# A hybrid decoder block on one Trainium2 core: order of the first loads, order of the weight splits at head 0, and the last rows in single-bank pieces

## The chip, the cores and the metric

The kernel runs on one core of one Trainium2 chip. The engines are named as in the profile: PE multiplies matrices (PEld loads its stationary operand), DVE and ACT work elementwise, POOL prepares small tiles, SP issues most transfers between device memory and SBUF. The metric is the device time of one launch in microseconds (us), the median of several runs; less is better.

## The reference

528 rows of tokens (16 fixed ones ahead of 512) of width 1024 pass one decoder block in float32. What is computed, cut to what matters:

```
u = rmsnorm(h); q, f, i, g, b, c, x, ga, gb = split(u @ w_in)
f = lb + (1 - lb) * sigmoid(f); k = 1 - f
o = hgrn2 recurrence over (silu(q), k, i, log f), 8 heads of 128
y_a = rmsnorm(o) * silu(g);  y_b = b * causal_conv(c * x)
h = h + (sigmoid(ga) * y_a + sigmoid(gb) * y_b) @ w_out
a, v = split(rmsnorm(h) @ w_up)
h = h + (silu(causal_conv(a) + bias) * v) @ w_down
out = rmsnorm(h)[16:]          # mean of squares over 1024, then * final_norm_w
```

## The kernel before

**Products in three parts.** Every float32 operand of a matmul is split on the chip into a high and a low part, and every product is three matmuls: high by high, high by low, low by high. For weights a **unit** (128 columns of w_in, all 1024 rows) is fetched by SP, cast to `wh` by ACT (line 100) and the rest `wl` is subtracted by DVE (line 101); `load_unit` does all of it. Later weights come as **pairs**, four blocks whose sums are used in a seven-product scheme (`pair_weights`, lines 287 to 323; the subtraction there is line 304, the additions 313, 314 and 318). That scheme also needs sums and differences of the tokens, which `combos` makes for the two halves of the contraction (jp 0 and 1): line 390 to 402 compute one (`ct`), ACT line 374 and DVE line 376 split it into `cm`. They are made a step at a time by a generator, which `some(n)` advances by n steps.

**Order.** The program is written in one stream; a framework orders the instructions of each engine from it, and each engine then works through its own queue in order, waiting by semaphores on the others.

**The start.** SP's queue fetches the parameters `par_t`, then quarters of the first two units (`heads`) and the eight token tiles `xt` in turn (lines 222 to 234). ACT scales a token tile to `uh` (line 165), DVE subtracts to `ul` (line 166), PE multiplies (lines 437 to 439). Line 173 squares the first token tile into `acc`, where the sum of squares of the tokens is gathered.

**Head 0.** After the units of head 0 the loop over `items` (lines 875 to 901) goes through what is left of the projections: first three single units of head 1, (f,1), (q,1) and (i,1), kind "s", then pairs (kind "p") and merges (kind "m"). A single unit is multiplied in two halves by `half_unit`; between them `some(99)` lets the generator of the combinations run to its end. Recurrence pieces of head 0 (lines 538 to 635) are put between the matmuls. Line 842 is a piece of the convolution, line 866 the result of (q,1).

**The end.** The down projection adds into the rows `HT` by groups of 128-wide pieces of the hidden width. For the last group of four (lines 1091 to 1111), each of four chunks of 128 rows has two halves q of 512 columns with twelve matmuls each (`down3`, lines 1044 to 1046). Both halves lie in one two-bank tile of PSUM:

```
ps = new_ps()
for q in range(2):
    o = ps[:, q * 512:(q + 1) * 512]
    ...
    dve.tensor_tensor(HT[c][q], o, HT[c][q], op=ALU.add)                      # 1098
    act.activation(junk, HT[c][q], AF.Square, accum_out=ss[:, c, q:q + 1])    # 1099
    dve.tensor_tensor(HT[c][q], HT[c][q], fw[q], op=ALU.mult)                 # 1100
dve.tensor_tensor(v, ss[:, c, :1], ss[:, c, 1:], op=ALU.add)                  # 1102
dve.tensor_scalar(v, v, 1.0 / D, EPS, op0=ALU.mult, op1=ALU.add)              # 1103
```

Then `rsqrt_of` makes the reciprocal root (lines 187 to 191), ACT and DVE scale the halves by it (lines 1108 and 1110), and SP writes them out.

Of the kernel before, what the change touches and what calls it, by code (L numbers as in the profile page):

```python
# [7 lines left out]
F32 = mybir.dt.float32  # L8
F32R = mybir.dt.float32r
I32 = mybir.dt.int32  # L10
AF = mybir.ActivationFunctionType
ALU = mybir.AluOpType
PSUM = bass.MemoryType.PSUM

P = 128
D = 1024
# [10 lines left out]
EPS = 1e-6  # L27
NCH = SEQ // P
# [29 lines left out]
def block_kernel(ctx: ExitStack, tc: tile.TileContext, xT, par, wts, pairs, ident, masks, finw, out):  # L58
    nc = tc.nc
    dve, act, pe = nc.vector, nc.scalar, nc.tensor  # L60
# [17 lines left out]
    def home(i, dtype=F32, n=528, name="t"):  # L78
        return big.tile([P, 528], dtype, name=f"{name}{i}", tag=f"b{i}")[:, :n]
# [6 lines left out]
    def fetch(parts=1):  # L86
        u = next_unit[0]
        next_unit[0] += 1
        raw = wpool.tile([P, KT, P], F32, name=f"wr{u}", tag="wr")
        n = KT // parts  # L90
        return raw, [lambda i=i: nc.sync.dma_start(raw[:, i:i + n, :], wts[u, :, i:i + n, :])
                     for i in range(0, KT, n)]

    def split_unit(raw, parts=1):
        h = whl.tile([P, KT, P], F32R, name="wh", tag="wh")
        lo = whl.tile([P, KT, P], F32R, name="wl", tag="wl")
        n = KT // parts

        def part(i):
            act.copy(h[:, i:i + n, :], raw[:, i:i + n, :])  # L100
            dve.tensor_tensor(lo[:, i:i + n, :], raw[:, i:i + n, :], h[:, i:i + n, :].bitcast(F32),  # L101
                              op=ALU.subtract)

        return h, lo, [lambda i=i: part(i) for i in range(0, KT, n)]

    def load_unit():
        raw, loads = fetch()
        h, lo, parts = split_unit(raw)
        loads[0]()
        parts[0]()  # L110
        return h, lo
# [27 lines left out]
    mains = []  # L139
    turn = [0]  # L140

    def new_ps():
        pool = mains[turn[0] // 2 % len(mains)]
        turn[0] += 1
        return pool.tile([P, 1024], F32, name="psm", tag="psm")
# [38 lines left out]
    def rsqrt_of(dst, v, pool, w, tag):  # L184
        y = pool.tile([P, w], F32, name=f"ry{tag}", tag=f"ry{tag}")
        t = pool.tile([P, w], F32, name=f"rt{tag}", tag=f"rt{tag}")
        act.activation(y, v, AF.Sqrt)
        dve.reciprocal(y, y)
        dve.tensor_tensor(t, y, v, op=ALU.mult)
        dve.scalar_tensor_tensor(t, t, -0.5, y, op0=ALU.mult, op1=ALU.mult)  # L190
        dve.scalar_tensor_tensor(dst, t, 1.5, y, op0=ALU.add, op1=ALU.mult)
# [28 lines left out]
    heads = [fetch(4) for _ in range(2)]  # L220

    def load_x(k):
        nc.sync.dma_start(xt[k], xT[k * P:(k + 1) * P, :])

    nc.sync.dma_start(par_t, par)
    heads[0][1][0]()
    load_x(0)
    heads[1][1][0]()
    load_x(1)
    for i in range(1, 4):  # L230
# [231 lines left out]
    with tc.tile_pool(name="rp0", bufs=1) as rp:  # L462
# [19 lines left out]
        ahead = [load_unit()]  # L482
# [156 lines left out]
    def ring(tag="z", bufs=3):  # L639
        return p2.tile([P, L], F32, name=tag, tag=tag, bufs=bufs)  # L640
# [123 lines left out]
    def value(j):  # L764
        return lambda o, at: act.copy(V_t[:, at], o)
# [47 lines left out]
    def some(n):  # L813
        for _ in range(n):
            next(work[0], None)
# [4 lines left out]
    s = ring()  # L820
# [33 lines left out]
    def forget(j):  # L854
        def sink(o, at):
            act.activation(Fs[j % 2][:, at], o, AF.Sigmoid)
            if at.start:
                keys(j)
        return sink
# [9 lines left out]
    items = [("s", forget(1)), ("s", lambda j=1: query(j)), ("s", value(1)), ("p", lambda: GA(0)), ("m", 0)]  # L869
# [6 lines left out]
    for q, (kind, arg) in enumerate(items):  # L876
        if kind == "m":
            if cur:
                cur.last()
                cur = None  # L880
            merge(arg)
            if arg + 1 < KT:
                beat[:] = [0, 6 if arg + 2 < KT else 4]
                begin(arg + 1)
        elif kind == "p":
            w = pair_weights()
            nxt = Pair(w, arg(), HL, lambda: None)
            if cur:
                cur.last()
            cur = nxt  # L890
            cur.middle()
        else:
            unit = ahead.pop() if ahead else load_unit()
            sink = arg() if arg.__name__ == "<lambda>" and arg.__code__.co_argcount == 1 else arg
            half_unit(unit, 0, sink)
            if cur:
                cur.last()
                cur = None
            some(99)
            half_unit(unit, 1, sink)  # L900
    some(99)

    ph.close()
    scan.close()
# [46 lines left out]
    with tc.tile_pool(name="rp1", bufs=1) as rp:  # L951
        acc = fp2.tile([P, LT], F32, name="acc", tag="fa")
        for k in range(KT):
            ps = mtile(mh, ml, LATE)
# [5 lines left out]
        ahead = load_unit()  # L960
        ps = new_ps()
# [20 lines left out]
    for q, (f, i) in enumerate(units):  # L982
        unit = ahead
        if q + 1 < len(units):
            ahead = load_unit()
# [11 lines left out]
    HT = [[xt[4 * q + c][:, :512] for q in range(2)] for c in range(NCH)]  # L997
# [31 lines left out]
    n = 0  # L1029
# [11 lines left out]
    def down3(o, g, c, w, first, last):  # L1041
        gh, gl = (x[:, c * P:(c + 1) * P] for x in gs[g])
        wh, wl = w
        pe.matmul(o, gh, wh, start=first, stop=False)  # L1044
        pe.matmul(o, gh, wl, start=False, stop=False)  # L1045
        pe.matmul(o, gl, wh, start=False, stop=last)  # L1046
# [32 lines left out]
        for _ in work:  # L1079
            pass  # L1080
    pairs_ps.close()
    mains.append(ctx.enter_context(tc.tile_pool(name="pmain2", bufs=2, space=PSUM)))

    fw = [home(24 + q, n=512, name="fw") for q in range(2)]
    for q in range(2):
        nc.scalar.dma_start(fw[q], finw[q * 512:(q + 1) * 512].partition_broadcast(P))
    tp = ctx.enter_context(tc.tile_pool(name="tp", bufs=1, side="right"))
    ss = tp.tile([P, NCH, 2], F32, name="ssf")
    junk = tp.tile([P, 512], F32, name="junkf")
    grp = spans[-1]  # L1090
    ws = [[down_block() for _ in grp] for q in range(2)]
    for c in range(NCH):
        ps = new_ps()
        for q in range(2):
            o = ps[:, q * 512:(q + 1) * 512]
            for g, w in zip(grp, ws[q]):
                down3(o, g, c, w, g == grp[0], g == grp[-1])
            dve.tensor_tensor(HT[c][q], o, HT[c][q], op=ALU.add)
            act.activation(junk, HT[c][q], AF.Square, accum_out=ss[:, c, q:q + 1])
            dve.tensor_tensor(HT[c][q], HT[c][q], fw[q], op=ALU.mult)  # L1100
        v = tp.tile([P, 1], F32, name="vf", tag="vf", bufs=2)
        dve.tensor_tensor(v, ss[:, c, :1], ss[:, c, 1:], op=ALU.add)
        dve.tensor_scalar(v, v, 1.0 / D, EPS, op0=ALU.mult, op1=ALU.add)
        rf = tp.tile([P, 1], F32, name="rf", tag="rf", bufs=2)
        rsqrt_of(rf, v, tp, 1, "f")
        for q in range(2):
            if q:
                act.activation(HT[c][q], HT[c][q], AF.Copy, scale=rf)
            else:
                dve.tensor_scalar(HT[c][q], HT[c][q], rf, None, op0=ALU.mult)  # L1110
            nc.sync.dma_start(out[c * P:(c + 1) * P, q * 512:(q + 1) * 512], HT[c][q])


def _masks():
# [64 lines left out]
```

## Time and profile before

| | |
|---|---|
| median of 3 runs | 881.46 us (880.99 to 881.69) |
| profiled execution | 881.89 us |
| span of its trace | 880.1 us |
| PE busy | 862.0 us (98%), 6984 matmuls |
| DVE busy | 717.9 us (82%), 1320 instructions |
| ACT busy | 528.9 us (60%), 1002 instructions |
| POOL busy | 34.6 us (4%) |

The span is counted from the first to the last record of the trace; 1.8 us of the execution lie around it. In the timelines a row has start, duration (both us), engine, line, operation, what is written and read by the program's names, sizes, and in brackets how long the engine was idle just before and what ended that. Matmuls overlap, so their pitch (from start to start) tells more than their duration. Names in rows: `pr`, `psm`, `psq` are tiles in PSUM, `wr` a raw weight unit, `wt` the rest of a pair, `hn` normed tokens, `cacc` the convolution, `xr` rows of `HT`, `vf` the mean of squares.

### The profile page before, as it was taken

The page shows a single profiled execution, that of the slowest core. Times are in us where ns is not written, and L with a number is a line of the kernel's source. Part 1 is how long each engine was busy: PE and PEld are TensorE (multiplying, and loading weights), DVE is VectorE, ACT ScalarE, POOL GpSimd, SP SyncE. Part 2 cuts the span into 40 slices and gives each one's busy share as a digit, 9 for nine tenths or more (in the row PEclk, how much of TensorE's full clock was granted, in tenths as well). Part 3 has the DMA queues.
Part 4 walks back from the last instruction along what each step waited for, and adds up shares of the span by engine and source line. Part 5 has one row for each costly group of instructions (what it writes and reads, how often), then busy time and mean ns, then how long its engine had stood idle before and what let it go on. Part 6 is the DMA issues. An engine that isn't in the chain of part 4 may idle for free.

```text
span 880.1 us, 17447 instructions
## 1 busy us (share of the span) xinstructions
PE 862.0 (98%) x6984; PEld 814.5 (93%) x6984; DVE 717.9 (82%) x1320; ACT 528.9 (60%) x1002; POOL 34.6 (4%) x110
## 2 busy tenths in 40 slices
PE   8989999999999999999999999999999999999995
PEld 8979999999999999999999999999999999999984
DVE  7899998988988889889986559976877787877665
ACT  8854777676776667776684346554545545455424
POOL 1220020100101001020000000000000000000000
PEclk9998999999999999999999999999999999999999
DMA  7316344343443434334335323533443534433202
GB/s 255 98 34 206 121 146 127 93 155 107 144 132 88 145 116 145 107 110 145 96 94 174 97 73 95 168 99 118 147 140 108 179 98 152 135 115 125 97 24 96
DMA packets 38817, 107.98 MB, mean 123 GB/s; under 512 B 4304, under 2 KB 5712, under 8 KB 38736
## 3 DMA queue, kind: packets, MB, share of 16 engines
q1 hardware_dynamic: 38448, 106.34, 38.2%
q8 instruction: 55, 0.90, 0.4%
q10 hardware_dynamic: 288, 0.52, 0.2%
q14 instruction: 26, 0.21, 0.1%
HBM read 104.75 MB, written 2.10 MB: 121 GB/s over the span
## 4 chain that ended last, share of the span: by engine, by line
PE 79%; DVE 12%; DMA 4%; ACT 3%; issue 1%; SPq 1%; DVEq 0%; ACTq 0%
PE pr L330 14%; PE pr L331 13%; PE pr L332 13%; PE psm L1044 5%; PE psm L1046 5%; PE psm L1045 5%; PE psm L123 4%; PE psm L120 4%; PE psm L121 4%; DMA wt<-in_pairs 4%; DVE wl L304 3%; PE pr L437 3%; PE pr L439 2%; PE pr L438 2%; PE psq L544 1%
## 5 line engine op out<-in xcount | busy, mean ns | idle before, releaser
L330 PE MATMUL pr<-cm,wh 128*128 128x264 f32 (+1 forms) x784 | 228.0, 292 | 1.1 <-ACT c L338 0.9
L331 PE MATMUL pr<-cm,wh 128*128 128x264 f32 (+1 forms) x784 | 222.6, 284 | 0.0
L332 PE MATMUL pr<-cm,wl 128*128 128x264 f32 (+1 forms) x784 | 222.3, 284 | 0.0
L330 PEld LDWEIGHTS pr<-cm,wh 128*128 128x128 f32 x784 | 147.4, 188 | 6.0 <-ACT c L338 2.7
L332 PEld LDWEIGHTS pr<-cm,wl 128*128 128x128 f32 x784 | 147.8, 189 | 0.0
L331 PEld LDWEIGHTS pr<-cm,wh 128*128 128x128 f32 x784 | 147.5, 188 | 0.0
L303 ACT CAST wh<-wt 128x1024 fp32r<-128x1024 f32 x88 | 92.7, 1053 | 74.2 <-PE pr L331 34.2
L304 DVE TENSOR_TENSOR wl<-wt,wh 128x1024 fp32r<-128x1024 f32 x88 | 107.1, 1217 | 30.2 <-ACT wh L303 30.2
L101 DVE TENSOR_TENSOR wl<-wr,wh 128x1024 fp32r<-128x1024 f32 (+1 forms) x64 | 71.7, 1123 | 38.6 <-ACT wh L100 37.2
L100 ACT CAST wh<-wr 128x1024 fp32r<-128x1024 f32 (+1 forms) x64 | 61.8, 969 | 67.7 <-PE psm L121 31.1
L330 PE MATMUL pr<-cf,wh 128*128 128x258 f32 x256 | 72.5, 283 | 0.0
L331 PE MATMUL pr<-cf,wh 128*128 128x258 f32 x256 | 72.1, 282 | 0.0
L332 PE MATMUL pr<-cf,wl 128*128 128x258 f32 x256 | 71.9, 281 | 0.0
L338 ACT COPY c<-pr 128x264 f32<-128x264 f32 (+1 forms) x132 | 49.4, 374 | 30.5 <-PE pr L332 22.1
L304 DVE TENSOR_TENSOR wl<-wr,wh 128x1024 fp32r<-128x1024 f32 x44 | 53.7, 1221 | 12.0 <-ACT wh L303 11.3
L303 ACT CAST wh<-wr 128x1024 fp32r<-128x1024 f32 x44 | 46.2, 1050 | 21.1 <-PE pr L331 19.6
L313 DVE TENSOR_TENSOR wt<-wt 128x1024 f32<-128x1024 f32 x44 | 53.6, 1219 | 4.9 <-DMA wt<-in_pairs 4.8
L330 PE MATMUL pr<-cb,wh 128*128 128x258 f32 x192 | 54.7, 285 | 0.3 <-ACT xr L1005 0.3
L331 PE MATMUL pr<-cb,wh 128*128 128x258 f32 x192 | 54.7, 285 | 0.0
L332 PE MATMUL pr<-cb,wl 128*128 128x258 f32 x192 | 54.4, 283 | 0.0
L331 PEld LDWEIGHTS pr<-cf,wh 128*128 128x128 f32 x256 | 48.6, 190 | 0.8
L330 PEld LDWEIGHTS pr<-cf,wh 128*128 128x128 f32 x256 | 48.1, 188 | 0.7
(298 smaller groups left out, 2241.1 us busy)
## 6 DMA issues: line engine op xcount, KB each, us to landing
wr<-in_wts SPq DMA_DIRECT2D x56, 512.0 KB, 3.6
wr<-in_pairs SPq DMA_DIRECT2D x44, 512.0 KB, 4.1
wt<-in_pairs SPq DMA_DIRECT2D x44, 512.0 KB, 4.0
wt<-in_pairs SPq DMA_DIRECT2D x88, 256.0 KB, 4.7
xt<-in_xT SPq DMA_DIRECT2D x8, 264.0 KB, 4.5
xr<-in_xT SPq DMA_DIRECT2D x8, 264.0 KB, 3.9
out<-xr SPq DMA_DIRECT2D x8, 256.0 KB, 2.2
wr<-in_wts SPq DMA_DIRECT2D x8, 128.0 KB, 4.3
```

The lines of the kernel that those rows point to most:

```text
L100: act.copy(h[:, i:i + n, :], raw[:, i:i + n, :])
L101: dve.tensor_tensor(lo[:, i:i + n, :], raw[:, i:i + n, :], h[:, i:i + n, :].bitcast(F32), op=ALU.subtract)
L303: act.copy(h, src)
L304: dve.tensor_tensor(lo, src, h.bitcast(F32), op=ALU.subtract)
L313: dve.tensor_tensor(t[:, 1:3, :], t[:, 1:3, :], t[:, 3:, :].to_broadcast([P, 2, 512]), op=ALU.add)
L330: pe.matmul(ps, h[:, j], ch, start=start and j == 0, stop=False, skip_group_check=True)
L331: pe.matmul(ps, h[:, j], cl, start=False, stop=False, skip_group_check=True)
L332: pe.matmul(ps, lo[:, j], ch, start=False, stop=j == 3, skip_group_check=True)
L338: act.copy(c, r)
L1044: pe.matmul(o, gh, wh, start=first, stop=False)
L1045: pe.matmul(o, gh, wl, start=False, stop=False)
L1046: pe.matmul(o, gl, wh, start=False, stop=last)
```

## The change

Four edits. (1) The first token tile is fetched first, then the first quarter of weights, and the parameters third. (2) In the loop over `items`, when the next item is a single unit too, that unit is loaded and split before the first half of the present one is multiplied; and the generator of the combinations is advanced by one step between the halves and, where a single unit follows, by one after them, instead of to its end. (3) At the end every piece has a single-bank tile of PSUM of its own from a pool of four, the second half of the last chunk is cut in two pieces of 256 columns, and the multiplication by the final weights writes to a new tile `z` instead of over the rows that are squared. (4) The argument of the root is accumulated in `vs`, one instruction a piece, in place of an addition and a scaling at the end.

```diff
@@ -222,9 +222,9 @@
     def load_x(k):
         nc.sync.dma_start(xt[k], xT[k * P:(k + 1) * P, :])
 
+    load_x(0)
+    heads[0][1][0]()
     nc.sync.dma_start(par_t, par)
-    heads[0][1][0]()
-    load_x(0)
     heads[1][1][0]()
     load_x(1)
     for i in range(1, 4):
@@ -891,14 +891,16 @@
             cur.middle()
         else:
             unit = ahead.pop() if ahead else load_unit()
+            if items[q + 1][0] == "s":
+                ahead.append(load_unit())
             sink = arg() if arg.__name__ == "<lambda>" and arg.__code__.co_argcount == 1 else arg
             half_unit(unit, 0, sink)
             if cur:
                 cur.last()
                 cur = None
-            some(99)
+            some(1)
             half_unit(unit, 1, sink)
-    some(99)
+            some(1 if items[q + 1][0] == "s" else 99)
 
     ph.close()
     scan.close()
@@ -1079,36 +1081,41 @@
         for _ in work:
             pass
     pairs_ps.close()
-    mains.append(ctx.enter_context(tc.tile_pool(name="pmain2", bufs=2, space=PSUM)))
+    pfin = ctx.enter_context(tc.tile_pool(name="pfin", bufs=4, space=PSUM))
 
     fw = [home(24 + q, n=512, name="fw") for q in range(2)]
     for q in range(2):
         nc.scalar.dma_start(fw[q], finw[q * 512:(q + 1) * 512].partition_broadcast(P))
     tp = ctx.enter_context(tc.tile_pool(name="tp", bufs=1, side="right"))
-    ss = tp.tile([P, NCH, 2], F32, name="ssf")
+    ss = tp.tile([P, NCH, 3], F32, name="ssf")
+    vs = tp.tile([P, NCH, 3], F32, name="vsf")
     junk = tp.tile([P, 512], F32, name="junkf")
     grp = spans[-1]
     ws = [[down_block() for _ in grp] for q in range(2)]
     for c in range(NCH):
-        ps = new_ps()
-        for q in range(2):
-            o = ps[:, q * 512:(q + 1) * 512]
+        z = [home(26 + 2 * c + q, n=512, name="zf") for q in range(2)]
+        pieces = [(0, 0, 512), (1, 0, 512)] if c + 1 < NCH else [(0, 0, 512), (1, 0, 256), (1, 256, 512)]
+        for at, (q, a, b) in enumerate(pieces):
+            o = pfin.tile([P, 512], F32, name="pf", tag="pf")[:, :b - a]
             for g, w in zip(grp, ws[q]):
-                down3(o, g, c, w, g == grp[0], g == grp[-1])
-            dve.tensor_tensor(HT[c][q], o, HT[c][q], op=ALU.add)
-            act.activation(junk, HT[c][q], AF.Square, accum_out=ss[:, c, q:q + 1])
-            dve.tensor_tensor(HT[c][q], HT[c][q], fw[q], op=ALU.mult)
-        v = tp.tile([P, 1], F32, name="vf", tag="vf", bufs=2)
-        dve.tensor_tensor(v, ss[:, c, :1], ss[:, c, 1:], op=ALU.add)
-        dve.tensor_scalar(v, v, 1.0 / D, EPS, op0=ALU.mult, op1=ALU.add)
+                down3(o, g, c, [x[:, a:b] for x in w], g == grp[0], g == grp[-1])
+            h = HT[c][q][:, a:b]
+            dve.tensor_tensor(h, o, h, op=ALU.add)
+            act.activation(junk[:, :b - a], h, AF.Square, accum_out=ss[:, c, at:at + 1])
+            dve.tensor_tensor(z[q][:, a:b], h, fw[q][:, a:b], op=ALU.mult)
+            if at:
+                dve.scalar_tensor_tensor(vs[:, c, at:at + 1], ss[:, c, at:at + 1], 1.0 / D, vs[:, c, at - 1:at],
+                                         op0=ALU.mult, op1=ALU.add)
+            else:
+                dve.tensor_scalar(vs[:, c, :1], ss[:, c, :1], 1.0 / D, EPS, op0=ALU.mult, op1=ALU.add)
         rf = tp.tile([P, 1], F32, name="rf", tag="rf", bufs=2)
-        rsqrt_of(rf, v, tp, 1, "f")
+        rsqrt_of(rf, vs[:, c, at:at + 1], tp, 1, "f")
         for q in range(2):
             if q:
-                act.activation(HT[c][q], HT[c][q], AF.Copy, scale=rf)
+                act.activation(z[q], z[q], AF.Copy, scale=rf)
             else:
-                dve.tensor_scalar(HT[c][q], HT[c][q], rf, None, op0=ALU.mult)
-            nc.sync.dma_start(out[c * P:(c + 1) * P, q * 512:(q + 1) * 512], HT[c][q])
+                dve.tensor_scalar(z[q], z[q], rf, None, op0=ALU.mult)
+            nc.sync.dma_start(out[c * P:(c + 1) * P, q * 512:(q + 1) * 512], z[q])
 
 
 def _masks():
```

How this moves instructions on the engines is seen at three places. On DVE, around line 842 while head 0's recurrence is under way; `wl<-wr_...` on line 101 is the low part of a single unit, `cm` a split combination, `Q`, `K`, `T` belong to the recurrence. Before, from line 842 on:

```order
L842 TENSOR_TENSOR cacc<-cacc,z 128x264
L538 TENSOR_TENSOR qv<-Q_238,T_893 128x8x16 x2
L376 TENSOR_TENSOR cm_816<-ct,cm_815 128x528
L540 TENSOR_TENSOR qv<-qv,T_893 128x8x16
L546 TENSOR_TENSOR Q_238<-Q_238,T_893 128x8x16
L547 TENSOR_TENSOR Q_238<-qv,T_893 128x8x16
L548 TENSOR_TENSOR Q_238<-qv,T_893 128x8x16
L553 TENSOR_TENSOR TK_968<-T_893 128x8
L398 SCALAR_TENSOR_TENSOR ct<-ct,hn 128x528
L554 TENSOR_TENSOR TK_968<-T_893,TK_968 128x8
L562 COPY_PREDICATED B_235<-mk_t,psq 128x4x48
L555 TENSOR_TENSOR T_969<-T_893,TK_968 128x8
```

and, with `wl` of unit (q,1) on its last row, up to the subtraction:

```order
L556 TENSOR_TENSOR K_227<-K_227,TK_968 128x8x48
L562 COPY_PREDICATED B_235<-mk_t,psq 128x4x32
L376 TENSOR_TENSOR cm_818<-ct,cm_817 128x528
L562 COPY_PREDICATED B_235<-mk_t,psq 128x4x16
L402 TENSOR_TENSOR ct<-hn 128x528
L390 TENSOR_TENSOR ct<-hn 128x528
L101 TENSOR_TENSOR wl<-wr_1041,wh 128x1024
```

After, the same place:

```order
L842 TENSOR_TENSOR cacc<-cacc,z 128x264
L101 TENSOR_TENSOR wl<-wr_926,wh 128x1024
L376 TENSOR_TENSOR cm_816<-ct,cm_815 128x528
L538 TENSOR_TENSOR qv<-Q_238,T_893 128x8x16 x2
L546 TENSOR_TENSOR Q_238<-Q_238,T_893 128x8x16
L540 TENSOR_TENSOR qv<-qv,T_893 128x8x16
L547 TENSOR_TENSOR Q_238<-qv,T_893 128x8x16
L548 TENSOR_TENSOR Q_238<-qv,T_893 128x8x16
L553 TENSOR_TENSOR TK_974<-T_893 128x8
L398 SCALAR_TENSOR_TENSOR ct<-ct,hn 128x528
```

Line 101 has moved from behind eighteen instructions to right behind line 842; the next one (unit (i,1)) follows after line 402 of the first half, and lines 390 to 402 of the second half come later still.

Also on DVE, in the first pairs, where `Q_239`, `TK` and `T` belong to head 1's recurrence, `F_230` on line 668 is a result of the pair for head 2 and line 101 the unit (i,2). Before, from the recurrence's second step:

```order
L538 TENSOR_TENSOR qv<-Q_239,T_1536 128x16x2x4 x2
L546 TENSOR_TENSOR Q_239<-Q_239,T_1536 128x32x4
L540 TENSOR_TENSOR qv<-qv,T_1536 128x16x8
L547 TENSOR_TENSOR Q_239<-qv,T_1536 128x32x4
L548 TENSOR_TENSOR Q_239<-qv,T_1536 128x32x4
L553 TENSOR_TENSOR TK_1609<-T_1536 128x32
```

After, where these now stand:

```order
L668 TENSOR_TENSOR F_230<-pr,c_1412 128x264
L101 TENSOR_TENSOR wl<-wr_1480,wh 128x1024
L655 SCALAR_TENSOR_TENSOR Q_238<-pr,c_1475 128x264
L556 TENSOR_TENSOR K_228<-K_228,TK_1535 128x128x3
L562 COPY_PREDICATED B_234<-mk_t,psq 128x32x3
L673 TENSOR_TENSOR Q_238<-Q_238,z 128x264
L562 COPY_PREDICATED B_234<-mk_t,psq 128x32x2
L538 TENSOR_TENSOR qv<-Q_239,T_1536 128x16x2x4
L562 COPY_PREDICATED B_234<-mk_t,psq 128x32
L538 TENSOR_TENSOR qv<-Q_239,T_1536 128x16x2x4
L546 TENSOR_TENSOR Q_239<-Q_239,T_1536 128x32x4
L540 TENSOR_TENSOR qv<-qv,T_1536 128x16x8
```

The recurrence's second step, which stood ahead of lines 731, 734 and 668, now follows line 668, line 101 and the first result of the next product.

On ACT at the start of the program; `acc` is the sum of squares, `uh` a scaled token tile, `wh` a quarter of weights. Before:

```order
L100 CAST wh<-wr_90 128x256
L165 ACTIVATE uh_210<-xt_80,par_t 128x528
L100 CAST wh<-wr_91 128x256
L165 ACTIVATE uh_211<-xt_81,par_t 128x528
L100 CAST wh<-wr_90 128x256
L100 CAST wh<-wr_91 128x256
L173 ACTIVATE acc<-xt_80 128x528
L165 ACTIVATE uh_212<-xt_82,par_t 128x528
```

After:

```order
L173 ACT_TABLE_LOAD
L173 ACTIVATE acc<-xt_80 128x528
L277 ACTIVATE lbe_191<-lbe_191 128x8
L278 ACTIVATE lbe_192<-lbe_192 128x8
L100 CAST wh<-wr_90 128x256
L165 ACTIVATE uh_210<-xt_80,par_t 128x528
L100 CAST wh<-wr_91 128x256
L165 ACTIVATE uh_211<-xt_81,par_t 128x528
L100 CAST wh<-wr_90 128x256
L165 ACTIVATE uh_212<-xt_82,par_t 128x528
```

The square on line 173 has moved from behind the fourth cast to the head of the queue, and `uh_212` stands directly behind the third cast.

## Rows read from the trace of the kernel before

**Rows 1.** Waits of PE: what for, us in total, times, longest.
```profile
PE pr L439 <- DVE wl L101: 3.2, 1, 3.2
...
PE psm L1044 <- DVE vf L1103: 1.1, 1, 1.1
```

**Rows 2.** Windows: stretch, us, busy of PE PEld DVE ACT POOL, PEclk, DMA.
```profile
64.00:68.00 4.00, 2.19 (x10) 2.19 (x11) 4.00 (x7) 1.82 (x4) 2.99 (x4) 0.65 0.72 172
68.00:72.00 4.00, 4.00 (x20) 4.00 (x20) 3.37 (x8) 1.83 (x4) 0.00 (x0) 0.50 0.69 231
58.00:80.00 22.00, 18.48 (x143) 17.47 (x142) 20.03 (x41) 12.67 (x33) 5.50 (x10) 0.84 0.48 144
80.00:104.00 24.00, 23.69 (x193) 23.03 (x191) 23.47 (x54) 18.84 (x42) 0.00 (x0) 1.00 0.48 151
130.00:160.00 30.00, 29.99 (x273) 29.11 (x272) 26.75 (x52) 21.03 (x47) 0.00 (x0) 1.00 0.41 129
```

**Rows 3.** Timeline of PE, 65 to 74 us.
```profile
65.81 0.59 PE L439 MATMUL pr<-cm,wl 128*128 128x264 f32 x1 [3.20 <-DVE wl L101]
...
71.91 0.33 PE L438 MATMUL pr<-cm,wh 128*128 128x264 f32 x1
72.08 0.28 PE L439 MATMUL pr<-cm,wl 128*128 128x264 f32 x1
...
73.54 0.28 PE L439 MATMUL pr<-cm,wl 128*128 128x264 f32 x1
```

**Rows 4.** Timeline of DVE, 57 to 72 and 93 to 98 us.
```profile
57.99 0.43 DVE L842 TENSOR_TENSOR cacc<-cacc,z 128x264 f32<-128x264 f32 x1
...
64.48 1.27 DVE L101 TENSOR_TENSOR wl<-wr,wh 128x1024 fp32r<-128x1024 f32 x1
...
70.08 0.70 DVE L402 TENSOR_TENSOR ct<-hn 128x528 f32<-128x528 f32 x1
...
71.47 0.43 DVE L866 TENSOR_TENSOR Q<-pr,z 128x264 f32<-128x264 f32 x1 [0.63 <-ACT z L865]
...
94.12 0.47 DVE L538 TENSOR_TENSOR qv<-Q,T 128x128 f32<-128x128 f32 x2
...
97.34 0.17 DVE L555 TENSOR_TENSOR T<-T,TK 128x8 f32<-128x8 f32 x1
```

**Rows 5.** Timeline of SP, one issue of a pair's transfer.
```profile
70.81 0.33 SPq L293 DMA_DIRECT2D wt<-in_pairs  x1
```

**Rows 6.** Chain that ended last: start, us, engine, tile, line.
```profile
868.57 0.60 DVE xr L1098
...
872.30 0.70 DVE xr L1098
...
873.09 0.73 ACT junkf L1099 x2
...
874.64 0.17 DVE vf L1103
...
875.84 0.72 ACT xr L1108
```

**Rows 7.** Timeline of PE, last matmuls of the end.
```profile
867.70 0.40 PE L1046 MATMUL psm<-wh,gs 128*128 128x512 f32 x1
...
871.88 0.39 PE L1046 MATMUL psm<-wh,gs 128*128 128x512 f32 x1
```

**Rows 8.** Timeline of ACT, start of the program and a 256-wide instruction.
```profile
8.14 0.64 ACT L173 ACTIVATE acc<-xt 128x528 f32<-128x528 f32 x1
8.69 1.35 ACT L165 ACTIVATE uh<-xt,par_t 128x528 fp32r<-128x528 f32 x2
...
53.91 0.41 ACT L840 ACTIVATE z<-z 128x256 f32<-128x256 f32 x1
```

**Rows 9.** Timeline of PE, start of the program.
```profile
10.26 0.39 PE L438 MATMUL pr<-ul,wh 128*128 128x264 f32 x1 [0.17 <-DVE ul L166]
```

## The prediction

> **What bounds the kernel now.** I read the list of waits of PE first, because PE is busy almost all the time and the only quick gains are where it stands still. It shows one long wait, 3.20 us for the low half of a weight unit (line 101), and one of 1.13 us near the end for line 1103 [rows 1]. Next come the windows. Between 64 and 72 us the clock granted to PE is 0.65 and then 0.50, which is the 1.2 GHz level, after the stretch in which PE stood; everywhere else that I use it is 1.00 [rows 2]. The same rows say that DVE is nearly full around this place: of the 46 us from 58 to 104 it is idle for (22.00 - 20.03) + (24.00 - 23.47) = 2.50 us, while from 130 to 160 it has 3.25 us to spare. The timeline of PE gives the price of the lower clock, a pitch of 0.22 us between matmuls instead of 0.12 [rows 3]. The timeline of DVE gives the reason for the wait: the subtraction on line 101 starts at 64.48, although what it needs was there long before; other work stands ahead of it in DVE's queue [rows 4]. Last I read the chain of waits at the end [rows 6] and the first ten microseconds [rows 8, 9].
>
> **Head 0 and the next unit.** PE stops at 62.61 (65.81 less 3.20) and before that for 0.33 us on line 578, so 3.53 us are idle. Then it runs slowly: from 65.81 to 71.91 lie 27 intervals that take 6.10 us; at the later pitch, 12 intervals in 73.54 - 72.08 = 1.46, that is 0.1217 each, they would take 3.29, so 2.81 us are lost to the clock [rows 3]. Together 6.34 us is the most that this place can return.
>
> In the changed order line 101 stands right behind line 842, which starts at 57.99 and takes 0.43; the subtraction itself took 1.27 [rows 4]. So it would be done at about 59.6. PE, kept at its pitch, comes to the first product with the low half at about 60.1 by my laying of the new order, and needs it 2.5 us sooner than it got as far before; it still arrives in time by half a microsecond. The second moved subtraction, for the unit after it, I lay at 66.1 against a need at 66.9.
>
> What moves back pays. Eighteen DVE instructions that stood ahead of line 101 now run behind it. They are the combinations of tokens and the first steps of head 0's recurrence, and they are wanted by PE later. Their delay can only be made good by DVE's idle time and by work that is put off past this stretch. The idle time is 2.50 us. The order of the change puts off twelve small instructions of head 1's recurrence, from line 538 at 94.12 to line 555 at 97.34, past line 668 and the next line 101; their durations add to 2.7 us [rows 4]. That makes 5.2 us. Laying both queues instruction by instruction with the durations of the trace I get four new short waits of PE, on lines 633, 668, 101 and 544, of about 0.4, 0.2, 0.5 and 0.2 us, 1.3 in all, and so 6.34 - 1.3 = 5.0 us. The two ways agree. I take **-5.1 us**, with 2.5 (only the idle time comes back) and 6.4 as bounds.
>
> One queue is passed by this: SP issues the transfer of the next pair's tiles at 70.81, once line 402 of the second half of the combinations has freed the buffer [rows 4, 5]. In the new order that line comes at about 75, so the tiles land some 5 us later. Before, the weights made from them were ready 9 us ahead of PE by my laying, so about 4 us of cover remain, and I cost this at nothing.
>
> **The end.** Before, the last twelve matmuls wait because the two halves of a chunk share one tile of two banks: the addition on line 1098 for the first half stands behind a multiplication that waits for the square, and PE waits for that addition, which ends at 869.17 (868.57 and 0.60) [rows 6]. From the first half's last matmul at 867.70 to the very last at 871.88 pass 4.18 us [rows 7]. With single-bank tiles the pieces follow at once: one 512-wide interval, about twice a 264-wide one's 0.12, and 23 of 256-wide matmuls. No row has that shape with these operands; by the 264-wide pitch of 0.1217 [rows 3] they take at most 0.12 each, so 23 x 0.12 = 2.76, in all 3.00. That is **-1.2 us**.
>
> From the last matmul's start to the start of the final scaling pass 875.84 - 871.88 = 3.96 us: 0.42 to the addition, the addition 0.70, the square with its sum 0.73, then 0.82 in which the multiplication and the addition of the two sums run, and 1.20 from line 1103 to the end of the root [rows 6]. In the change the piece is 256 wide, the multiplication writes to a tile of its own and the square does not hold it up, and the addition of the two sums and the scaling are one instruction. I take 0.31 to the addition (a matmul of 0.28 against one of 0.39 [rows 3, 7]), 0.43 for the addition (a 264-wide one from PSUM took that) [rows 4], 0.08, 0.51 for the square (a 256-wide ACT instruction took 0.41 [rows 8], and 0.10 for the sum), 0.02 and the same 1.20. That is 2.55, so **-1.4 us**. The tail gives 2.6, between 2.2 (the multiplication still on the path at part of its length) and 2.9 (the square's halves as good as the addition's).
>
> The rows price the narrow pieces too: a 512-wide addition takes 0.70 and a 264-wide one 0.43, so two halves cost 0.16 more than one whole [rows 4, 6]. Only the second half lies behind the last matmul, the first runs under 12 matmuls of 0.12, so on the path the split saves 0.27. The Trainium skill, "VectorE: DVE Perf Modes", section "The TRN2 errata — SBUF-src ops pay a fixed extra latency per instruction", speaks against it: every instruction pays a fixed latency, and it advises tiles of at least 512 elements. By that advice alone, with the first half's cost not hidden, the tail would be worth about 2.4 instead of 2.6.
>
> **The start.** PE's last break there ends at 10.26 [rows 9]. On ACT the square on line 173, 0.55 us from its start to the next one's, stands in the chain that leads to it, between a cast of weights and the scaling of a token tile [rows 8]. The change takes it to the front of ACT's queue, and fetches the first token tile before the weights. If the chain simply shortens, 0.55 us come back; on the other side, the square now stands ahead of the first cast and the first scaled tile, so the first product may begin up to 0.5 later, and the parameters are fetched third. I take **-0.4 us**, from -0.6 to +0.4.
>
> **Sum.** -5.1 - 2.6 - 0.4 = -8.1 us. The profiled execution took 881.89 us, of which 880.1 are the span and 1.8 lie around it. It gives 873.8; it stands 0.43 us above the median of 881.46, and against that median the forecast is 881.46 - 8.1 = **873.4 us**.
>
> **Rivals.**
> - *DVE is the bound.* If the put-off work of head 1 is missed soon after, PE waits for it and only DVE's idle 2.50 us is won: -2.5 - 2.6 - 0.4 = -5.5, 876.0 us. For it: DVE is 98% busy from 80 to 104. Against it: 3.25 idle us from 130 to 160 [rows 2]. Chance 0.18.
> - *The start gives nothing or costs 0.3:* 881.46 - 5.1 - 2.6 + 0.3 = 874.1. Chance 0.10.
> - *The end doesn't do what it says:* the pieces still wait for a bank because DVE's queue comes late to the addition, and the 1.2 us stay: 874.6. Chance 0.06.
> - *Slower.* The put-off line 402 holds the transfer of the pair's tiles. If PE reaches the product that needs them before they are split, it stands, and after such a stop the clock falls to the lower level, which cost 2.81 us the last time. That takes away 4 us of cover first; to lose all of the 8.1 us the wait must reach some 5.3 us, so the tiles must land over 9 us later than I lay them. For it: SP's queue is full of large transfers. Against it: the margin. At that point the time is 881.5, beyond it slower; I allow 0.06, half of it for each side.
> - *As forecast:* 0.60, with a range of its own from 872.0 to 875.0.
>
> **How the numbers follow.** A measurement of this kernel can tell about 0.2%, 1.8 us, from no change. Only the late-transfer case comes that near: slower 0.03, same 0.03, faster 0.94. The range takes in the first three rivals with the bounds of the terms: low 881.46 - 6.4 - 2.9 - 0.6 = 871.6, high 881.46 - 2.5 - 2.2 + 0.4 = 877.2, so **871.5 to 877.2**.
>
> **What would show it.** Right: no wait of PE for line 101 above 0.6 us, a granted clock of 1.00 from 64 to 72, no wait at the last chunk, about 2.6 us from the last matmul to the final scaling. Wrong: a clock of 0.5 anywhere between 60 and 104, a wait of PE above 1 us on lines 544 to 668 or on a pair's weights between 80 and 100, or a first unbroken run of PE that begins after 10.3.

## The result, and the profile after

| | before | after |
|---|---|---|
| median | 881.56 us (880.99 to 881.69, 4 runs) | 873.35 us (872.90 to 874.32, 4 runs) |
| ratio | | 0.9913, 95% interval 0.9899 to 0.9927 |
| profiled execution | 881.89 us | 872.90 us |
| span of its trace | 880.1 us | 871.1 us |
| PE busy | 862.0 us (98%) | 859.1 us (99%) |

The change made the kernel 8.2 us faster by the medians (6.4 to 8.9 by the interval of the ratio); forecast were 8.1. The sum came out, but none of its three terms did, and that their errors cancel to 0.1 us is luck. In the list of PE's waits in the changed kernel (us in total, times, longest) the waits for line 101 and for the last chunk [rows 1] are gone, and at its head stands a longer wait at the start.

```profile
PE pr L437 <- ACT uh L165: 1.4, 1, 1.4
PE pm L635 <- DVE om L629: 1.2, 3, 0.6
...
PE psq L633 <- ACT on L628: 0.7, 1, 0.7
```

To see where the 9.0 us between the two profiled executions come from, the same matmul is looked for in both traces and the two starts are subtracted. The first matmul on line 544, before head 0's place, started at 47.41 and now at 48.30: 0.9 late. The first of the first pair (line 330) moved from 80.95 to 75.60, 5.4 early. The last matmul of the last pair went from 836.86 to 830.91, 6.0 early, and the final scaling from 875.84 to 866.88, 9.0 early. So the start lost 0.9, head 0's place won 6.2, the long middle 0.6 and the end 3.0. The 0.6 of the middle lies within the scatter: from the first matmul on line 544 to the last on line 330 the eight profiled executions that have the second part of the change whole (after, `e2_items`, `e4_nostart` to `e8_in_place`, `e12_changed_again`) took 781.9 to 784.6 us, the three without it (before, `e1_start`, `e3_end`) 789.2 to 790.1.

**Head 0's place.** Windows of the changed kernel (stretch, us, busy of PE, PEld, DVE, ACT, POOL, granted clock, DMA) that answer to [rows 2], and line 101 in DVE's timeline, that answers to [rows 4]:

```profile
64.00:68.00 4.00, 4.00 (x38) 3.79 (x38) 3.99 (x9) 2.26 (x6) 3.26 (x6) 1.00 0.17 43
68.00:72.00 4.00, 4.00 (x35) 3.99 (x34) 3.80 (x9) 2.50 (x6) 0.00 (x0) 1.00 0.94 277
...
58.00:80.00 22.00, 22.00 (x195) 21.01 (x194) 21.34 (x47) 15.79 (x40) 4.98 (x10) 1.00 0.41 125
80.00:104.00 24.00, 24.00 (x249) 23.23 (x248) 23.89 (x56) 18.54 (x42) 0.00 (x0) 1.00 0.54 171
...
124.00:154.00 30.00, 29.07 (x238) 28.23 (x236) 29.18 (x60) 21.04 (x48) 0.00 (x0) 1.00 0.46 142
130.00:160.00 30.00, 29.07 (x292) 28.17 (x291) 29.13 (x70) 21.04 (x45) 0.00 (x0) 1.00 0.40 123
```

```profile
59.21 1.21 DVE L101 TENSOR_TENSOR wl<-wr,wh 128x1024 fp32r<-128x1024 f32 x1
...
65.99 1.21 DVE L101 TENSOR_TENSOR wl<-wr,wh 128x1024 fp32r<-128x1024 f32 x1
```

Both subtractions come 5 us or more earlier than before, where they started at 64.48 and 71.83. PE does not stand in the 46 us from 58 to 104, and the clock stays at 1.00. DVE's idle time there fell from 2.50 to 0.77 us. The stretch from 130 to 160 is where it is paid: DVE went from 26.75 to 29.13 us busy (29.18 from 124 to 154, where the same work lies now that it comes some 6 us earlier), and PE lost 0.93 us, 0.74 of it in the wait on line 633. That wait names ACT, but ACT's line 628 had itself waited for DVE:

```profile
137.82 1.14 ACT L628 ACTIVATE on<-po,rs 128x128 f32<-128x128 f32 x4 [0.39 <-DVE rs L191]
138.24 0.33 PE L633 MATMUL psq<-id_t,on 128*128 128x128 f32 x1 [0.74 <-ACT on L628]
```

**The end.** PE's last matmuls in the changed kernel, that answer to [rows 7], and the end of its chain, that answers to [rows 6]:

```profile
861.34 0.39 PE L1048 MATMUL pf<-wh,gs 128*128 128x512 f32 x1
...
864.29 0.28 PE L1048 MATMUL pf<-wh,gs 128*128 128x256 f32 x1
```

```profile
864.70 0.35 DVE xr L1103
...
865.13 0.52 ACT junkf L1104 x2
...
865.67 0.17 DVE vsf L1107
...
866.88 0.72 ACT zf L1115
```

The 24 narrow matmuls take 864.29 - 861.34 = 2.95 us where 4.18 were, and from the last one to the final scaling pass 866.88 - 864.29 = 2.59 where 3.96 were. The chain counts the addition on line 1103 only from the end of the instruction ahead of it; in DVE's timeline it takes 0.42 us:

```profile
864.62 0.42 DVE L1103 TENSOR_TENSOR xr<-pf,xr 128x256 f32<-128x256 f32 x1
```

**The start.** ACT's timeline in the changed kernel, and PE's:

```profile
3.41 0.64 ACT L173 ACTIVATE acc<-xt 128x528 f32<-128x528 f32 x1 [1.40 <-DMA xt<-in_xT]
5.64 0.21 ACT L277 ACTIVATE lbe<-lbe 128x8 f32<-128x8 f32 x1 [1.59 <-DVE lbe L275]
5.76 0.19 ACT L278 ACTIVATE lbe<-lbe 128x8 f32<-128x8 f32 x1
5.86 0.39 ACT L100 CAST wh<-wr 128x256 fp32r<-128x256 f32 x1
6.15 0.73 ACT L165 ACTIVATE uh<-xt,par_t 128x528 fp32r<-128x528 f32 x1
```

```profile
6.93 1.25 PE L437 MATMUL pr<-uh,wh 128*128 128x264 f32 x4 [1.43 <-ACT uh L165]
7.98 0.42 PE L438 MATMUL pr<-ul,wh 128*128 128x264 f32 x1
...
9.96 0.36 PE L438 MATMUL pr<-ul,wh 128*128 128x264 f32 x1
10.15 0.28 PE L439 MATMUL pr<-uh,wl 128*128 128x264 f32 x1
```

The first token tile lands early, and its square is done at 4.05. Then ACT stands for 1.59 us: the exponential on line 277 waits by way of DVE for the parameters, and the first cast and the first scaled tile stand behind it in ACT's queue. The first product begins at 6.93 instead of 5.83, and PE then works at a pitch of 0.22 us until 9.96, that of the lower clock [rows 3]. The pitch alone shows this; the clock column of the windows says 1.00 there. PE did not fall to the lower level at this place, it had not left it: the 40 small matmuls that run first (line 245) keep a pitch of 0.11 us to their end in this execution, while in the kernel before the pitch halves at 3.7 us. Here are both, first the kernel before:

```profile
1.05 3.67 PE L245 MATMUL pm<-ones 128*128 128x128 bf16 x40 [1.05 <-DVE ones L241]
```

```profile
1.06 4.45 PE L245 MATMUL pm<-ones 128*128 128x128 bf16 x40 [1.06 <-DVE ones L241]
```

That is not the work of the new order, for with the old one they take 4.45 us in `e3_end` and `e4_nostart` too.

### The profile page after: what moved, and what is told of

Same layout as the page of the kernel before. It is cut to its first block, busy times and chain, and to the rows that moved or that the text cites. A ratio compares the mean times of both kernels' runs of the same rounds, so it can differ in the third digit from the quotient of the medians.

```text
span 871.1 us, 17481 instructions
## 1 busy us (share of the span) xinstructions
PE 859.1 (99%) x6996; PEld 814.5 (93%) x6996; DVE 717.5 (82%) x1323; ACT 529.3 (61%) x1004; POOL 37.5 (4%) x110
## 4 chain that ended last, share of the span: by engine, by line
PE 80%; DVE 12%; ACT 4%; DMA 3%; issue 1%; SPq 0%; DVEq 0%; ACTq 0%
PE pr L330 14%; PE pr L331 13%; PE pr L332 13%; PE psm L123 4%; PE psm L120 4%; PE psm L121 4%; PE psm L1048 4%; PE psm L1047 4%; PE psm L1046 4%; PE pr L437 3%; DVE wl L304 3%; PE pr L438 3%; PE pr L439 3%; DMA wt<-in_pairs 2%; PE psq L544 1%
```

## The experiments

All comparisons in time are with the kernel before on the same chip, and with the changed kernel by way of the ratios; single runs of a kernel lie up to 3.3 us from its median, so what is below 1 us is read from the traces.

**Each part alone.** Three kernels with one part of the change each on the kernel before, and one with all but the first part.

`e1_start`:

```diff
-    nc.sync.dma_start(par_t, par)
-    heads[0][1][0]()
     load_x(0)
+    heads[0][1][0]()
+    nc.sync.dma_start(par_t, par)
```

> Only the first edit (first token tile, then weights, then parameters). Theory from the two traces: the parameters land at about 5.2 us instead of 2.7, the two exponentials that wait for them stand ahead of the first cast and the first scaled tile on ACT, and the first product begins about 1.1 us later; 0.7 to 0.9 us of it remain when the tokens' sum of squares is multiplied near 22 us, so slower than before by 0.7 to 0.9 us. Rival, the term of the prediction: 0.4 us faster. Rival two: the loss is made good before the end, within 0.2 us of before.

Measured: 882.67 us, ratio 1.0012 (0.9999 to 1.0024), about 1 us slower, between 0.1 faster and 2.1 slower. The first product began at 6.32, the first matmul on line 544 at 47.48, in this execution only 0.07 later than before: PE reached the product with the sum of squares 0.6 us early and waited 0.63 us for it.

`e2_items`:

```diff
+            if items[q + 1][0] == "s":
+                ahead.append(load_unit())
...
-            some(99)
+            some(1)
             half_unit(unit, 1, sink)
-    some(99)
+            some(1 if items[q + 1][0] == "s" else 99)
```

> Only the second edit (split of the next unit ahead, combinations a step at a time). Theory: the wait of 3.2 us for line 101 and the stretch at half clock go, the first product of the first pair starts 6.0 to 6.4 us earlier than before, some of it is given back near 130 to 150 us when head 1's put-off recurrence is wanted, and the end is 6 to 7 us earlier. Rival, DVE is the bound: 2.5 us earlier. Rival, the prediction's term: 5.1 us.

Measured: 875.02 us, ratio 0.9932 (0.9916 to 0.9948), so 6.0 us faster, 4.6 to 7.4. The first pair began at 74.65, 6.3 us earlier than before, and PE waited 0.5 us on line 633 at 137. The rival by which only DVE's idle 2.5 us come back falls.

`e3_end` is the last two hunks of the change alone:

```diff
+    pfin = ctx.enter_context(tc.tile_pool(name="pfin", bufs=4, space=PSUM))
...
+        z = [home(26 + 2 * c + q, n=512, name="zf") for q in range(2)]
+        pieces = [(0, 0, 512), (1, 0, 512)] if c + 1 < NCH else [(0, 0, 512), (1, 0, 256), (1, 256, 512)]
...
```

> Only the third and fourth edits (end of the kernel). Theory: 3.0 us faster (1.6 in PE's last group: the wait of 1.13 with the slower pieces around it, and 0.4 of short pauses at the starts of chunks; 1.4 from the last matmul to the final scaling). The prediction's term: 2.6 us.

Measured: 878.18 us, ratio 0.9969 (0.9958 to 0.9980), 2.7 us faster, 1.8 to 3.7; its profiled span is 877.1 against 880.1. The three parts add to +1.0 - 6.0 - 2.7 = -7.7 us, what the ratio of the whole change gives too.

`e4_nostart` is the changed kernel with the first three loads as before (the diff of `e1_start` read backwards).

> The changed kernel with the first loads as before (parameters, weights, first token tile). Theory: 0.7 to 0.9 us faster than the changed kernel, so about 872.5 us and a first product at about 5.8 us. Rival, the prediction's term: 0.4 us slower than the changed kernel, 873.8 us. Rival two: the same as the changed kernel within 0.2 us.

Measured: 873.43 us, ratio 0.9907 (0.9891 to 0.9923); the changed kernel has 0.9913. In time the two can't be told apart. In the trace all of it comes earlier: the first product at 5.58, the first on line 544 at 47.07, the end of the span at 870.2 instead of 871.1.

**The first loads in other orders.** Two more orders, both on the changed kernel.

`e5_par_second`:

```diff
     load_x(0)
-    heads[0][1][0]()
     nc.sync.dma_start(par_t, par)
+    heads[0][1][0]()
```

> The changed kernel with the parameters second: first token tile, parameters, first weights. Theory (the parameters' late landing is what holds ACT): they land by about 4.0 us instead of 5.2, the first product begins at 5.0 to 5.8 us instead of 6.9, and the product with the sum of squares, near 22.6 in the changed kernel, comes at 21.0 to 21.8; 0.5 to 1 us faster than the changed kernel. Rival (the square at the head of ACT's queue is what costs): the first product stays later than 6.3 us.

`e6_par_act`:

```diff
+    nc.scalar.dma_start(par_t, par)
     load_x(0)
     heads[0][1][0]()
-    nc.sync.dma_start(par_t, par)
```

> The changed kernel with the parameters on ACT's own DMA queue, the first token tile and the weights first on SP. Theory: parameters land by about 3 us, the first scaled tile is made when the first token tile lands at about 3.5, the first product begins at 4.5 to 5.5 us, and the product with the sum of squares comes at 20.8 to 21.6 us; 0.8 to 1.5 us faster than the changed kernel. Rival: from 8 to 20 us ACT and DVE are full and the tiles arrive no sooner, so that product still comes at 21.6 or later and the gain over the first loads of before is nothing.

Measured: 873.91 us, 0.9909 (0.9893 to 0.9926), and 873.21 us, 0.9906 (0.9891 to 0.9921). With the parameters second the exponential stood no longer, it ran at 4.08, and the first product began at 5.38; so the late parameters were what held ACT, and not the square ahead of it. But nothing came of it: PE then stood for 0.53 us for the second cast, it waited 0.65 us for the sum of squares, whose product came at 22.12 (before 21.89), and the first matmul on line 544 came at 47.89. On ACT's queue the order of ACT's instructions changed: the first scaled tile went to the head, with the load of its table (1.28 us) behind the wait for the tile, the first product began only at 6.58, and the one with the sum of squares at 23.47. Both expectations of a gain fell.

`e12_changed_again` is the changed kernel, run beside the next one.

> The changed kernel once more, on the chip of the run beside it. Theory (the start costs 0 to 0.9 us with the landing of the first transfers, from one execution to the next): median 873.0 to 874.0 us, a first product between 6.2 and 7.0 us in its profile. Rival (the start gains 0.4 us): a first product before 6.0 us.

Measured: 874.07 us, 0.9916 (0.9900 to 0.9933), a first product at 7.12, both just above what was expected. Taken together: in the four profiled executions with the parameters first (before, `e2_items`, `e3_end`, `e4_nostart`) the first matmul on line 544 started at 47.41, 47.36, 47.34 and 47.07, on average 47.30; in the seven with the changed loads (after, `e1_start`, `e7_no_cut`, `e8_in_place`, `e9_all_steps`, `e10_no_ahead`, `e12_changed_again`) at 47.48 to 48.98, on average 48.26. In these traces the first part of the change costs about 1 us. Its size goes with how long PE works at the lower pitch there. In the changed kernel, `e9_all_steps` and `e12_changed_again` a stretch of it follows the first product, and line 544 comes at 48.30, 48.62 and 48.98; these are windows of `e12_changed_again`, where the clock had risen and fell again (granted clock 0.70 and 0.50):

```profile
8.00:10.00 2.00, 2.00 (x12) 2.00 (x13) 1.31 (x4) 1.16 (x3) 0.00 (x0) 0.70 1.03 370
10.00:12.00 2.00, 2.00 (x11) 2.00 (x10) 2.00 (x5) 2.00 (x6) 0.00 (x0) 0.50 1.06 298
```

But the pitch is not the whole loss. In `e7_no_cut`, `e8_in_place` and `e10_no_ahead` no such stretch follows, and line 544 still comes at 48.10 to 48.21: there PE waits 0.65 to 0.67 us for the sum of squares, whose product comes at 22.37 to 22.47, while before it waited 0.13 and went on at 21.89 (in `e1_start` it went on at 21.73, and there nothing was lost). What makes that sum late no run isolates. From 10 to 20 us DVE is busy for 9.90 us and ACT for 9.94 in the kernel before, so a likely reason, not a shown one, is that work which they get later cannot be made good there.

**What limits the start.** `e11_pool_sums` is `e4_nostart` with six of the seven additions of the tokens' squares on POOL; the last one stays on DVE.

```diff
-            dve.tensor_tensor(acc, acc, sq, op=ALU.add)
+            (nc.gpsimd if k < 7 and n == L else dve).tensor_tensor(acc, acc, sq, op=ALU.add)
```

> The changed kernel with the first loads as before, and the seven additions of the tokens' squares (0.70 us each on DVE between 11 and 21 us) on POOL. Theory (the stretch from 10 to 21 us is set by DVE's and ACT's queues, which is why the order of the first loads gives nothing): DVE has 4.9 us less to do there, and the product with the sum of squares comes at 20.5 to 21.3 us instead of 21.6; up to 1 us faster than the changed kernel with the first loads as before. Rival (POOL takes 1.5 us or more for an addition and slows DVE, or ACT's casts are the bound): that product at 21.6 or later, no gain or a loss of up to 2 us.

Measured: 876.72 us, 0.9951 (0.9933 to 0.9970), 3 us slower than the changed kernel. The answer on line 177 (durations shortest, median, longest in ns; first and last start) and DVE's timeline:

```profile
L177 POOL TENSOR_TENSOR acc<-acc,sq x6: 1366/1436/1678, 11.4 to 20.1; 128x528 f32<-128x528 f32 x6
```

```profile
9.56 1.45 DVE L166 SCALAR_TENSOR_TENSOR ul<-xt,par_t,uh 128x528 fp32r<-128x528 f32 x2 [1.05 <-ACT uh L165]
...
17.00 3.56 DVE L166 SCALAR_TENSOR_TENSOR ul<-xt,par_t,uh 128x528 fp32r<-128x528 f32 x2
```

An addition takes 1.44 us on POOL for 0.70 on DVE, and while POOL adds, two subtractions on DVE take 3.56 us for the 1.45 that they took just before POOL began. PE waited 2.7 us for line 166, and the product with the sum of squares came at 23.50. So the relief of DVE was turned into its opposite, and whether DVE's queue sets the time from 10 to 21 us stays open. The Trainium skill, "SBUF — State Buffer", section "SBUF: two separate sides", says that DVE and GpSimd share a pair of ports which one instruction holds to its end, among others a DVE instruction with two operands in SBUF; the trace goes the same way (1.78 us each instead of 0.72), though it shows no port, and waiting for a whole addition of 1.44 each time would come to 2.16.

**The end in pieces.** `e7_no_cut`:

```diff
-        pieces = [(0, 0, 512), (1, 0, 512)] if c + 1 < NCH else [(0, 0, 512), (1, 0, 256), (1, 256, 512)]
+        pieces = [(0, 0, 512), (1, 0, 512)]
```

> The changed kernel with the last piece not cut in two. Theory: from the start of the last 512-wide matmul before the last piece to the final scaling 5.9 us instead of 5.54 (0.35 more: the last addition 0.70 for 0.35 to 0.43, the square 0.73 for 0.52, less 0.2 of waiting on DVE). Rival (narrow pieces cost what they save): the same within 0.1 us.

The end of its chain, with the last matmul at 866.16:

```profile
866.59 0.70 DVE xr L1103
...
867.37 0.73 ACT junkf L1104 x2
...
869.34 0.72 ACT zf L1115
```

From the last matmul to the final scaling pass 3.18 us. Twelve 512-wide matmuls at 0.23 lie between that matmul and the one that the changed kernel has at 861.34: 3.18 + 12 x 0.23 = 5.94 against 866.88 - 861.34 = 5.54. The cut is worth 0.4 us, as expected. This kernel and the next ran once each (875.44 and 874.88 us), so only their traces are compared.

`e8_in_place`:

```diff
-        z = [home(26 + 2 * c + q, n=512, name="zf") for q in range(2)]
+        z = HT[c]
```

> The changed kernel with the multiplication by the final weights written over the rows, as before, so that it waits for the square. Theory: PE has no wait at the last chunk all the same, since the pieces have four single-bank tiles, but the multiplication stands between the square and the root: 0.4 to 0.7 us more from the last matmul to the final scaling than the 2.59 of the changed kernel. Rival (the separate tile is what frees PE): a wait of PE of 0.3 us or more in the last group.

The end of its chain, with the last matmul at 865.73:

```profile
866.77 0.52 ACT junkf L1104 x2
...
867.31 0.42 DVE xr L1105
...
868.86 0.72 ACT xr L1115
```

868.86 - 865.73 = 3.13 us, 0.54 more than 2.59: the multiplication stands behind the square and ahead of the root. PE has no wait in the last group. So the single-bank tiles, four of them, free PE, and the separate tile shortens what comes after it.

**Head 0 in pieces.** `e9_all_steps`:

```diff
-            some(1)
+            some(99)
             half_unit(unit, 1, sink)
```

> The changed kernel with all steps of the combinations run at once between the halves, as before; the next unit is still split ahead. Theory (the split ahead is what matters): the first unit's line 101 stays right behind line 842, the second moves back by one instruction of 0.65 us; no wait of PE for line 101 above 0.5 us, clock 1.00, first product of the first pair within 0.5 us of the changed kernel's. Rival (the steps matter as much): a wait of 2 us or more for line 101 and a stretch at half clock, 3 to 5 us slower.

Measured: 875.05 us, 0.9925 (0.9908 to 0.9941): 1 us slower than the changed kernel, within the intervals. There is no wait for line 101 and the clock is 1.00; PE has two new waits of 0.5 and 0.6 us at 72 and 74 us, for ACT. Its first matmul on line 330 moved ahead of other work, to 72.27, and can't be compared; the 200th comes 0.7 us later than in the changed kernel, both counted from the first on line 544 (128.5 and 127.8 us).

`e10_no_ahead`:

```diff
-            if items[q + 1][0] == "s":
-                ahead.append(load_unit())
```

> The changed kernel without the split ahead, with the combinations a step at a time. Theory: line 101 of the unit stands sixteen instructions behind line 842, 0.65 us sooner than before, so PE waits about 2.5 us for it and runs some 5 us at half clock after; 4.5 to 5.5 us slower than the changed kernel. Rival (the steps alone do it): within 1 us of the changed kernel.

Measured: 877.33 us, 0.9953 (0.9938 to 0.9968), 3.5 us slower than the changed kernel, less than expected. The wait is there, 2.52 us, but the clock did not fall behind it. Here are the matmul that waited and the windows after it, and below the same of `e1_start`, where line 101 stood as before and PE waited 3.37 us:

```profile
65.82 0.39 PE L439 MATMUL pr<-cm,wl 128*128 128x264 f32 x1 [2.52 <-DVE wl L101]
...
64.00:68.00 4.00, 2.18 (x18) 2.19 (x19) 4.00 (x8) 1.77 (x6) 3.10 (x5) 1.00 0.54 138
68.00:72.00 4.00, 4.00 (x36) 3.99 (x35) 4.00 (x6) 1.99 (x5) 0.00 (x0) 1.00 0.97 316
```

```profile
66.03 0.59 PE L439 MATMUL pr<-cm,wl 128*128 128x264 f32 x1 [3.37 <-DVE wl L101]
...
64.00:68.00 4.00, 1.97 (x9) 1.98 (x10) 4.00 (x7) 1.81 (x5) 3.20 (x5) 0.53 0.63 159
68.00:72.00 4.00, 4.00 (x23) 4.00 (x23) 3.40 (x8) 1.90 (x4) 0.00 (x0) 0.62 0.70 238
```

So without the split ahead 3.5 of the second part's 6 us are lost, without the steps about 1, within the intervals; the two are not additive. The steps alone shorten the wait from 3.2 to 2.5 us, and in this one profiled execution that was enough to keep the clock up; of the other three of `e10_no_ahead` there are no traces.

## Why the prediction was right, and where it was not

The time, 873.4 us forecast and 873.35 measured, came out of two terms that were too small and one with the wrong sign. The mechanisms of the two large terms held; the agreement to 0.1 us is luck.

- **Head 0's place, -5.1.** The mechanism was as forecast: the wait and the slow stretch are gone, and DVE's work that stood ahead was put off. The term was mis-sized by 0.6 to 1.1 us: -6.2 in the profile at the first pair, and -5.7 behind the wait on line 633 (the 200th matmul on line 330 started at 180.92 and now at 176.11, that is 133.5 and 127.8 us behind the first on line 544). In time it is -6.0 in `e2_items`, and the interval, 4.6 to 7.4, holds the forecast too. The step that failed is that of the four short new waits, 1.3 us. Of them the one on line 633 came, 0.74 us and at 137 instead of inside the stretch; lines 668 and 101 made PE wait for nothing, and the one on line 544 was there before (0.24, now 0.25). Putting the work off carried further than to line 668: DVE's spare time from 130 to 160 took it, where it fell from 3.25 to 0.87 us.
- **The transfers that the change holds back.** The tiles issued at 70.81 before [rows 5] are issued at 76.58, 5.8 us later, about as laid (5), and no wait of PE names them. The cover held, and the slower side with it.
- **The end, -2.6.** In the profile -3.0. The two parts that were priced came out at 1.23 (forecast 1.2) and 1.37 (1.4). Missed was 0.4 us of short pauses at the starts of the earlier chunks, which the list of waits doesn't show: from the first matmul of the last group, 848.14 before and 842.19 after, to that at 867.70 and 861.34 passed 19.56 and now 19.15 us. The narrow pieces paid 0.4 us, not 0.27. The 0.27 was the addition alone, and it came out, 0.42 for 0.70; the shorter square (0.52 for 0.73) and a shorter way from the last matmul to the addition (0.33 for 0.43) won another 0.3, and the 24 narrow matmuls gave 0.19 back, 2.95 for the 2.76 of twelve wide ones. Two narrow additions do cost more than a wide one, 0.84 for 0.70, about as priced; but the first of them lay under matmuls, so the advice against narrow tiles did not decide.
- **The start, -0.4.** The sign was wrong: the traces have a loss of about 1 us at line 544. The step that failed is "If the chain simply shortens, 0.55 us come back", with "PE's last break there ends at 10.26" as the point to which the start was followed. The break did go: in the changed kernel PE runs without one from 6.93 to line 544, so the sign of being wrong, a run that begins after 10.3, did not show either. But it was no gain: where PE came through sooner, as in `e1_start`, it waited for the sum of squares 10 us later. On the other side I priced the square and named the parameters that are fetched third, but not what waits for them. They landed 3.6 us after their issue instead of 1.9, and by lines 277 and 278 held all of ACT's queue, so the first product came 1.1 us late where "up to 0.5" was laid. That is not the whole cause: in `e5_par_second` the first product came at 5.38, sooner than before, and the product with the sum of squares was 0.2 us late all the same and line 544 0.5. What makes the sum late stays open.
- Only the rival on the start came near what happened; it had 0.3 us for it, and a chance of 0.10.

No run beat the changed kernel clearly: `e4_nostart`, which keeps the parameters first, ends 0.9 us earlier in its profile, but its median does not tell it apart.

## What to carry to other kernels

An operand that one engine makes for a waiting matmul belongs ahead of work that is only wanted later, even if that work has to be done too; what counts is where the engine has spare time afterwards, and here that was more than 60 us further on. When a transfer is moved back in a queue, look for the instruction that waits for it first and for everything behind that instruction in its engine's queue, not only for the operand that one has in mind. And follow a start to the next place where the engine waits: here neither an earlier first product nor a break that went away was time won. A sum that comes out right can hide terms that are wrong: only runs of each part alone showed it.

## What the runs showed of the hardware

While PE stood for 3.20 to 3.37 us (before, `e1_start`, `e3_end`) the granted clock fell to the 1.2 GHz level before PE worked again (a mean of 0.90, 0.73 and 0.86 over the pause), and it stayed there for another 5 to 6 us; in `e10_no_ahead`, with 2.52 us of standing and the same work around it, it stayed at 2.4 GHz. At the start of the program the time at which the higher level comes differs from execution to execution: the 40 small matmuls on line 245 took 3.67 us in the kernel before and 4.45 in the changed one, which had the pitch of the lower level until 9.96. In `e12_changed_again` the clock rose, PE stood for 1.61 us, and the clock fell to 0.50 again, after PE had gone on. An addition of 128x528 on POOL took twice what it takes on DVE (1.44 and 0.70 us), and a pair of DVE's subtractions beside it up to 2.5 times its usual time (3.56 and 1.45 us).
